# A transformer block kernel: first two mixers and the convolution part read each unit's sum from one PSUM bank, and GpSimd subtracts nothing

## The chip, the core and the metric

The kernel runs on one core of a Trainium2 chip, in one launch. The metric is device microseconds of that core; lower is better. Four compute engines work beside each other: PE (TensorE, the matrix engine, with its weight loads PEld beside its matmuls), DVE (VectorE), ACT (ScalarE) and POOL (GpSimd). SP (SyncE) issues the DMAs. Each engine runs its own instructions in order and waits on semaphores of the others. SBUF is the large on-chip memory; PSUM is the small one into which PE accumulates, used here as eight banks of 128 x 512 fp32.

## The reference, cut

256 tokens of width 1024 pass through two blocks. The first is a mixer (a pooling mixer, a chunked mLSTM with a short causal convolution, and a block attention side by side) and then a feed-forward net whose two halves pass a causal convolution over time:

```python
def causal_dwconv(x, w):
    xp = jnp.pad(x, ((0, 0), (K - 1, 0), (0, 0)))
    y = xp[:, 0:S] * w[0]
    for j in range(1, K):
        y = y + xp[:, j:j + S] * w[j]
    return y
# feed-forward, convolution part:  z = x @ w_up                  1024 -> 2 x 2816
#   h = silu(causal_dwconv(z)[gate]) * causal_dwconv(z)[up];  y = h @ w_down
```

The second block is two layers, each a gated feed-forward net (2816 wide, no convolution), a mixer (NSA attention in the first layer, HGRN in the second) and another gated feed-forward net. Everything is fp32, and nearly all of the work is products of the 256 tokens with weights that are used once.

## The kernel before

**Units.** All weights stream from HBM in units of 1 MB (`units`, made by `a_units` and `b_units`): 128 partitions x 8 x 256 or 2 x 1024 numbers. `get()` hands the next half unit to PE; by then units are loaded three ahead on SP's queue and halves split up to `ahead[0]` (5) ahead (`do_split`). Splitting writes a half as two numbers of reduced precision: ACT copies raw to `hi` (L264) and `lo = raw - hi` is a subtraction (L267) on DVE, or on POOL for the halves in `pool_halves`: five of the first mixer (table FP), every fifth of the convolution part and its last two (CF, CP), and the NSA mixer's last ones (`on_pool`), 30 in all. The hi buffers are six, the lo buffers three for each side, the raw buffers three.

**Products.** The activations XT are kept split as well, hi and lo side by side. There are two ways to multiply a kind "A" unit, whose weights are stationary:

- `gA` gives each half unit a PSUM bank of its own. For each of 8 slices k there is one matmul of hi weights on 512 columns (activations hi and lo) and one of lo weights on 256. The bank then holds two partial sums. `evA` (L434 to L445) adds them: ACT copies one to SBUF (`evs`, L441), DVE adds it to the other and writes z in SBUF (L442; with a scale L444 and L445). So a unit takes 32 matmuls, two banks and four evictions.
- `gZ`, used before in the HGRN mixer alone, gives both halves of a unit one bank. For each k there are three matmuls of 256 columns (lo weights on hi activations, hi on hi, hi on lo), all summed in PSUM. So a unit takes 48 matmuls and one bank, and whoever needs z reads the bank. Both pass through `bulk_mm` (L355).

PSUM tags psa and psb have two banks each; psS and psT have the other four.

**Where units are used.** In `first_mix`, `qk_m` multiplies two units and runs the mLSTM's short convolution on z (L704 to L706), `bulk_p` one and `bulk_a` two; `mmN` (L471) multiplies a narrow strip of gate weights in a psa bank. In `ffn` with conv=True each of ten iterations j takes a gate unit (psa) and an up unit (psb), then two halves of w_down (`mmD`, accumulators `acc`, 24 matmuls). `conv_z` runs three DVE operations on each half of z (L607 to L609), ACT takes Silu (L658), DVE multiplies (`times`, L626), and the product is split into H (L500 on ACT, L503 on DVE). At j = 0 the products have another form and the same three operations read a psS bank. At j = 10 `barrier` orders the following DVE subtractions behind `times`. In `nsa_mix`, `blocks` uses two units, `keys` two (ACT writes KH from z at L1112, DVE writes KL = z - KH at L1113, four of each), `bulk_q` four, later split in the same way into QS (L1136, L1137). Products L1097 go to psT banks and DVE reads them at L1100 (`vblk`).

**Order.** Each mixer's products run as generators that `drive` mixes with the small chains of attention and mLSTM; a scheduler then orders each engine's instructions. What stands in an engine's queue is fixed before the run.

Of the kernel before, what the change touches and what calls it, by code (L numbers as in the profile page):

```python
# [104 lines left out]
def _kern(ctx, tc, nc, A, out):  # L105
# [79 lines left out]
    for j in range(2):  # L185
        a_units(W, 1288 + 256 * j, 1)
        a_units(W, 1800 + 256 * j, 1, "B")
        a_units(W, 2312 + 256 * j, 1, "B")
    pool_halves.update(FP)
    b_units(A["w_out"], [0, 1, 2, 3])  # L190
    n0 = len(units)
    ffn_units(A["w_up"], 0, A["w_up"], DFF, A["w_down"], 2, 2)
    pool_halves.update(range(2 * n0 + CF[0], 2 * len(units) - 6, CF[1]))
    pool_halves.update(2 * len(units) + h for h in CP)
    for li in range(2):
        ffn_units(A["ffn1_w_gate_2"][li], 0, A["ffn1_w_up_2"][li], 0, A["ffn1_w_down_2"][li])
        if li == 0:
            W = A["nsa_w_in_2"]
            a_units(W, 1792, 1, "B")
            a_units(W, 2304, 1, "B")  # L200
            a_units(W, 1024, 2)
            a_units(W, 1536, 1)
            for kv in range(2):
                unit("c", kv, [16, 128])
            a_units(W, 2048, 1)
            narrow(W, 2560, 48)
            a_units(W, 0, 4)
            on_pool(len(units) - 9)
            b_units(A["nsa_w_out_2"], [0, 1, 2, 3])
        else:  # L210
            W = A["hgrn_w_in_2"]
            for j in range(4):
                for part in (1, 0, 3, 2) if j else (3, 2, 1, 0):
                    a_units(W, 1024 * part + 256 * j, 1, "A" if part < 2 else "B")
            b_units(A["hgrn_w_out_2"], [0, 1, 2, 3])
        ffn_units(A["ffn2_w_gate_2"][li], 0, A["ffn2_w_up_2"][li], 0, A["ffn2_w_down_2"][li])
# [379 lines left out]
    def ffn(XT, conv, half, finish):  # L596
        with tc.tile_pool(name=nm("ff"), bufs=2) as fp:
# [12 lines left out]
                return y  # L610

            def z_of(pool, ps, c0):
                return conv_z(evA(pool, ps, tag="cz", bufs=2), c0) if conv else evA(pool, ps)

            def turn(src):

# [18 lines left out]
            for j in range(11):  # L635
                sg = fp.tile([P, 2, 256], F32, tag="sg", name=nm("sg"))
                h = sg
                if j == 0:
                    pg, pu = mmB_first(XT)
                if j == 0 and conv:  # L640
                    zs = []
                    for n, ps in enumerate((pg, pu)):
                        zt = fp.tile([P, 2, 256], F32, tag="cz", bufs=2, name=nm("zt"))
                        for tt in range(2):
                            ACT.activation(zt[:, tt], ps[tt][:, 0:256], AF.Copy)
                        zs.append(conv_z(turn(zt), 22 * n))
                    ACT.activation(sg, zs[0], AF.Silu)
                    times(h, sg, zs[1])
                elif j == 0:
                    for tt in range(2):  # L650
                        ACT.activation(sg[:, tt], pg[tt][:, 0:256], AF.Silu)
                        times(sg[:, tt], sg[:, tt], pu[tt][:, 0:256])
                    h = turn(sg)
                else:
                    if conv and j == 10:
                        ahead[0] = SPL
                    zg = z_of(fp, mmA(XT), 2 * j)
                    ACT.activation(sg, zg, AF.Silu)  # L658
                    i = times(h, sg, z_of(fp, mmA(XT, psb), 22 + 2 * j))
                    if conv and j == 10:  # L660
                        barrier.append(i)
                H = fp.tile([P, 2, 2, 2, P], F32R, tag="H", bufs=2 + lag, name=nm("H"))
                split_to(H[:, :, :, 0, :], H[:, :, :, 1, :], h.rearrange("p c (t x) -> p c t x", t=2))
                ahead[0] = 5
                if j == 1:
                    acc = [new_acc(0), new_acc(1)]
                Hs.append(H)
                down(j - lag)
# [10 lines left out]
    def first_mix(XT, MT, W):  # L679
        with tc.tile_pool(name="m1", bufs=1) as mp:  # L680
# [6 lines left out]
            def qk_m():  # L687
# [9 lines left out]
                relative_bias(mp, rb)  # L697
                mT = []
                for u in range(2):
                    z = evA(mp, (yield from gA(XT)), tag="t2", bufs=4)  # L700
                    y = mp.tile([P, 2, 256], F32, tag="t2", bufs=4, name=nm("my"))
                    for c in range(2):
                        w = [vecs["m_conv"][:, 4 * j + 2 * u + c : 4 * j + 2 * u + c + 1] for j in range(4)]
# [14 lines left out]
                yield  # L718

            def bulk_p():  # L720
                ps = yield from gA(XT)
                d["zp"] = zp = mp.tile([P, 2, 272], F32, tag="zp", name="zp")
                POOL.memset(zp[:, :, 0:16], 0.0)
                evA(mp, ps, out=zp[:, :, 16:272])

            def bulk_a(u):
                d["zq", u] = zq = evA(mp, (yield from gA(XT)), tag="zq", bufs=2)

                sq = mp.tile([P, 2, 256], F32, tag="t2", bufs=4, name=nm("asq"))
                ACT.activation(sq, zq, AF.Square, scale=0.125)  # L730
# [290 lines left out]
    def nsa_mix(XT, MT, W):  # L1021
        with tc.tile_pool(name="m2", bufs=1) as mp:
# [20 lines left out]
            def blocks():  # L1043
# [8 lines left out]
                    for tt in range(2):  # L1052
                        ACT.activation(vv[br][:, tt], pss[br][tt][:, 0:256], AF.Copy)
                for kv in range(2):
                    z = evA(mp, (yield from gA(XT)), tag="zq", bufs=2)
                    blk = mp.tile([P, 16, 2, 2, 15], F32, tag="QS", bufs=2, name=nm("blk"))
                    for r in range(2):
                        rs = slice(64 * r, 64 * r + 64)
# [46 lines left out]
            KL = mp.tile([P, 4, 2, 256], F32R, name="KL")  # L1105

            def keys(br):
                z = evA(mp, (yield from gA(XT)), tag="zq", bufs=2)
                for r in range(2):
                    rs = slice(64 * r, 64 * r + 64)  # L1110
                    for o in (r, 1 - r):
# [12 lines left out]
                yield  # L1124

            def bulk_q(u):
                d["zq", u] = evA(mp, (yield from gA(XT)), scale=0.125, tag="zq", bufs=2)


            def group(u):  # L1130
# [455 lines left out]
```

## Time and profile before

| | before |
|---|---|
| median of 3 runs | 1419.66 us (1418.48 to 1422.54) |
| the profiled execution | 1419.54 us |
| its span, first to last instruction | 1417.7 us |
| granted TensorE clock, mean | 0.989 |
| PE busy | 1373.5 us, 97% |
| PEld busy | 1194.8 us, 84% |
| DVE busy | 971.8 us, 69% |
| ACT busy | 734.9 us, 52% |
| POOL busy | 116.6 us, 8% |

Starts and lengths are microseconds from the span's start. A line such as L267 is a line of the kernel before. "psa<-XT,hi" says that the operation writes a psa tile and reads XT and hi. Matmuls overlap, so their own durations add up to more than the time they take; the distance from one start to the next is the pace. "[6.26 <-DVE vblk L1100]" behind a row would be idle time of the engine ahead of it and what ended it. The granted clock is 1.00 at 2.4 GHz and 0.50 at 1.2 GHz.

### The profile page before, as it was taken

The page shows a single profiled execution, that of the slowest core. Times are in us where ns is not written, and L with a number is a line of the kernel's source. Part 1 is how long each engine was busy: PE and PEld are TensorE (multiplying, and loading weights), DVE is VectorE, ACT ScalarE, POOL GpSimd, SP SyncE. Part 2 cuts the span into 40 slices and gives each one's busy share as a digit, 9 for nine tenths or more (in the row PEclk, how much of TensorE's full clock was granted, in tenths as well). Part 3 has the DMA queues.
Part 4 walks back from the last instruction along what each step waited for, and adds up shares of the span by engine and source line. Part 5 has one row for each costly group of instructions (what it writes and reads, how often), then busy time and mean ns, then how long its engine had stood idle before and what let it go on. Part 6 is the DMA issues. An engine that isn't in the chain of part 4 may idle for free.

```text
span 1417.7 us, 20750 instructions
## 1 busy us (share of the span) xinstructions
PE 1373.5 (97%) x8121; PEld 1194.8 (84%) x8121; DVE 971.8 (69%) x1647; ACT 734.9 (52%) x1218; POOL 116.6 (8%) x95
## 2 busy tenths in 40 slices
PE   7899999998999999799999999999999999999997
PEld 6688888887888889688888888888889998888886
DVE  5865799997655776676855676665676666765574
ACT  5554554544555644576655564555555443645561
POOL 1320221220000003500000000000000000100000
PEclk9999999999999999899999999999999999999999
DMA  7523756654656665421555665555664442565560
GB/s 231 184 93 123 261 187 201 206 178 150 207 184 201 209 205 162 167 94 42 194 193 179 193 223 177 180 194 191 209 207 155 126 143 90 174 199 192 179 207 30
DMA packets 185425, 245.31 MB, mean 173 GB/s; under 512 B 7408, under 2 KB 164761, under 8 KB 185327
## 3 DMA queue, kind: packets, MB, share of 16 engines
q1 hardware_dynamic: 184511, 240.74, 52.0%
q0 software_dynamic: 816, 3.25, 0.6%
q8 instruction: 64, 1.05, 0.3%
q14 instruction: 34, 0.28, 0.1%
HBM read 242.89 MB, written 4.23 MB: 174 GB/s over the span
## 4 chain that ended last, share of the span: by engine, by line
PE 50%; issue 6%; DVE 1%; ACT 1%; POOL 1%; DVEq 0%; POOLq 0%; ACTq 0%
PE psa L355 19%; PE acc L355 13%; PE psb L355 12%; PE psb L1235 1%; PE psb L513 1%; PE psb L1237 0%; POOL rsr L536 0%; PE psT L1218 0%; PE psS L1189 0%; PE lev L1379 0%; PE psT L1220 0%; PE psb L1180 0%; PE psS L1147 0%; PE psS L1191 0%; ACT hi L264 0%
## 5 line engine op out<-in xcount | busy, mean ns | idle before, releaser
L267 DVE TENSOR_TENSOR lo<-raw,hi 128x1024 fp32r<-128x1024 f32 x398 | 492.5, 1243 | 252.2 <-ACT hi L264 251.1
L264 ACT ACTIVATE hi<-raw 128x1024 fp32r<-128x1024 f32 x428 | 448.5, 1055 | 330.2 <-PE psa L355 144.8
L355 PE MATMUL psa<-XT,hi 128*128 128x512 f32 (+1 forms) x1264 | 410.9, 375 | 3.2 <-DVE z L442 3.0
L355 PE MATMUL psa<-XT,lo 128*128 128x256 f32 x1136 | 322.2, 284 | 0.0
L355 PE MATMUL psb<-XT,hi 128*128 128x512 f32 x800 | 282.3, 393 | 0.0
L355 PE MATMUL acc<-hi,H 128*128 128x512 f32 x880 | 281.1, 392 | 0.0
L355 PEld LDWEIGHTS psa<-XT,hi 128*128 128x128 f32 x1264 | 230.3, 189 | 48.5 <-DVE z L442 4.2
L355 PE MATMUL psb<-XT,lo 128*128 128x256 f32 x800 | 223.3, 279 | 0.0
L355 PEld LDWEIGHTS psa<-XT,lo 128*128 128x128 f32 x1136 | 214.8, 189 | 3.8 <-issue 1.5
L355 PE MATMUL psa<-hi,XT 128*128 128x256 f32 (+1 forms) x928 | 197.4, 302 | 0.4 <-ACT XT L500 0.3
L355 PEld LDWEIGHTS acc<-hi,H 128*128 128x128 f32 x880 | 165.9, 189 | 35.3
L355 PEld LDWEIGHTS psb<-XT,hi 128*128 128x128 f32 x800 | 149.9, 187 | 35.9 <-DVE z L442 0.2
L355 PE MATMUL acc<-lo,H 128*128 128x512 f32 x440 | 173.8, 395 | 3.7 <-DVE lo L267 3.7
L355 PEld LDWEIGHTS psa<-hi,XT 128*128 128x128 f32 x928 | 150.8, 192 | 6.2 <-ACT XT L500 1.9
L355 PEld LDWEIGHTS psb<-XT,lo 128*128 128x128 f32 x800 | 149.9, 187 | 0.0
L355 PE MATMUL psa<-lo,XT 128*128 128x256 f32 (+1 forms) x464 | 131.2, 300 | 0.2 <-DVE lo L267 0.2
L355 PEld LDWEIGHTS acc<-lo,H 128*128 128x128 f32 x440 | 83.2, 189 | 20.8 <-DVE lo L267 4.1
L267 POOL TENSOR_TENSOR lo<-raw,hi 128x1024 fp32r<-128x1024 f32 x30 | 81.1, 2715 | 192.1 <-ACT hi L264 167.4
L355 PEld LDWEIGHTS psa<-lo,XT 128*128 128x128 f32 x464 | 89.4, 193 | 3.1 <-issue 1.0
L536 POOL TENSOR_TENSOR rsr<-var,mhalf 128x1 f32<-128x1 f32 x12 | 7.8, 647 | 796.5 <-ACT jk L574 796.5
L442 DVE TENSOR_TENSOR z<-psa,evs 128x256 f32<-128x256 f32 x116 | 48.3, 418 | 16.2 <-ACT evs L441 15.9
L500 ACT ACTIVATE H<-sg 128x512 fp32r<-128x512 f32 x51 | 31.7, 622 | 48.4 <-DVE sg L626 33.8
(350 smaller groups left out, 1294.5 us busy)
## 6 DMA issues: line engine op xcount, KB each, us to landing
raw<-in_ffn_w_gate_dram SPq DMA_DIRECT2D x44, 1024.0 KB, 5.1
raw<-in_ffn_w_up_dram SPq DMA_DIRECT2D x44, 1024.0 KB, 5.1
raw<-in_ffn_w_down_dram SPq DMA_DIRECT2D x44, 1024.0 KB, 4.9
raw<-in_w_up_dram SPq DMA_DIRECT2D x22, 1024.0 KB, 5.0
raw<-in_hgrn_w_in_dram SPq DMA_DIRECT2D x16, 1024.0 KB, 5.2
raw<-in_w_down_dram SPq DMA_DIRECT2D x11, 1024.0 KB, 4.9
raw<-in_nsa_w_in_dram SPq DMA_DIRECT2D x10, 1024.0 KB, 5.0
raw<-in_w_in_dram SPq DMA_DIRECT2D x9, 1024.0 KB, 5.1
```

The lines of the kernel that those rows point to most:

```text
L264: h = ACT.activation(hi, src, AF.Copy)
L267: i = (POOL if j in pool_halves else V).tensor_tensor(lo, src, hi.bitcast(F32), ALU.subtract)
L355: i = PE.matmul(o, l, r, start=start, stop=stop)
L442: V.tensor_tensor(zc, p4[:, :, 0, :], s, ALU.add)
L500: i = ACT.activation(hi, src, AF.Copy)
L513: ts = [PE.transpose(ps[:, j * P : (j + 1) * P], x[:, (q + j) * P : (q + j + 1) * P], ident) for j in range(w)]
L536: POOL.tensor_tensor(r[:, :n], src, mhalf[:, :n], ALU.pow)
L1235: PE.matmul(po5[:, 1, j % 2, br], T1[:, 2 * br + sb], vv[br][:, sb, vs], start=(sb == 0), stop=(sb == 1))
```

## The change

`pool_halves` stays empty: the 30 subtractions on POOL run on DVE. The five "A" units of the first mixer, the twenty of the convolution part and the eight of NSA (blocks, keys, bulk_q) go through `gZ` in place of `gA`, and `evA` is gone for them. Where z is used at once (mLSTM's convolution, `conv_z`, blocks, keys), DVE and ACT read the bank; in `bulk_p`, `bulk_a` and `bulk_q` one ACT copy of 128 x 512 takes z to SBUF. The gated feed-forward nets keep `gA` and `evA`. Behind L190 the changed kernel's line numbers are smaller by 1 to 4 (L355 is L351 there, L267 is L263).

```diff
@@ -186,12 +186,9 @@
         a_units(W, 1288 + 256 * j, 1)
         a_units(W, 1800 + 256 * j, 1, "B")
         a_units(W, 2312 + 256 * j, 1, "B")
-    pool_halves.update(FP)
     b_units(A["w_out"], [0, 1, 2, 3])
     n0 = len(units)
     ffn_units(A["w_up"], 0, A["w_up"], DFF, A["w_down"], 2, 2)
-    pool_halves.update(range(2 * n0 + CF[0], 2 * len(units) - 6, CF[1]))
-    pool_halves.update(2 * len(units) + h for h in CP)
     for li in range(2):
         ffn_units(A["ffn1_w_gate_2"][li], 0, A["ffn1_w_up_2"][li], 0, A["ffn1_w_down_2"][li])
         if li == 0:
@@ -205,7 +202,6 @@
             a_units(W, 2048, 1)
             narrow(W, 2560, 48)
             a_units(W, 0, 4)
-            on_pool(len(units) - 9)
             b_units(A["nsa_w_out_2"], [0, 1, 2, 3])
         else:
             W = A["hgrn_w_in_2"]
@@ -610,7 +606,7 @@
                 return y
 
             def z_of(pool, ps, c0):
-                return conv_z(evA(pool, ps, tag="cz", bufs=2), c0) if conv else evA(pool, ps)
+                return conv_z(ps, c0) if conv else evA(pool, ps)
 
             def turn(src):
 
@@ -654,9 +650,10 @@
                 else:
                     if conv and j == 10:
                         ahead[0] = SPL
-                    zg = z_of(fp, mmA(XT), 2 * j)
+                    mm = (lambda alloc: run(gZ(XT, alloc))) if conv else (lambda alloc: mmA(XT, alloc))
+                    zg = z_of(fp, mm(psa), 2 * j)
                     ACT.activation(sg, zg, AF.Silu)
-                    i = times(h, sg, z_of(fp, mmA(XT, psb), 22 + 2 * j))
+                    i = times(h, sg, z_of(fp, mm(psb), 22 + 2 * j))
                     if conv and j == 10:
                         barrier.append(i)
                 H = fp.tile([P, 2, 2, 2, P], F32R, tag="H", bufs=2 + lag, name=nm("H"))
@@ -697,7 +694,7 @@
                 relative_bias(mp, rb)
                 mT = []
                 for u in range(2):
-                    z = evA(mp, (yield from gA(XT)), tag="t2", bufs=4)
+                    z = yield from gZ(XT)
                     y = mp.tile([P, 2, 256], F32, tag="t2", bufs=4, name=nm("my"))
                     for c in range(2):
                         w = [vecs["m_conv"][:, 4 * j + 2 * u + c : 4 * j + 2 * u + c + 1] for j in range(4)]
@@ -718,13 +715,15 @@
                 yield
 
             def bulk_p():
-                ps = yield from gA(XT)
+                ps = yield from gZ(XT)
                 d["zp"] = zp = mp.tile([P, 2, 272], F32, tag="zp", name="zp")
                 POOL.memset(zp[:, :, 0:16], 0.0)
-                evA(mp, ps, out=zp[:, :, 16:272])
+                ACT.activation(zp[:, :, 16:272], ps, AF.Copy)
 
             def bulk_a(u):
-                d["zq", u] = zq = evA(mp, (yield from gA(XT)), tag="zq", bufs=2)
+                ps = yield from gZ(XT)
+                d["zq", u] = zq = mp.tile([P, 2, 256], F32, tag="zq", bufs=2, name=nm("zq"))
+                ACT.activation(zq, ps, AF.Copy)
 
                 sq = mp.tile([P, 2, 256], F32, tag="t2", bufs=4, name=nm("asq"))
                 ACT.activation(sq, zq, AF.Square, scale=0.125)
@@ -1052,7 +1051,7 @@
                     for tt in range(2):
                         ACT.activation(vv[br][:, tt], pss[br][tt][:, 0:256], AF.Copy)
                 for kv in range(2):
-                    z = evA(mp, (yield from gA(XT)), tag="zq", bufs=2)
+                    z = yield from gZ(XT)
                     blk = mp.tile([P, 16, 2, 2, 15], F32, tag="QS", bufs=2, name=nm("blk"))
                     for r in range(2):
                         rs = slice(64 * r, 64 * r + 64)
@@ -1105,7 +1104,7 @@
             KL = mp.tile([P, 4, 2, 256], F32R, name="KL")
 
             def keys(br):
-                z = evA(mp, (yield from gA(XT)), tag="zq", bufs=2)
+                z = yield from gZ(XT)
                 for r in range(2):
                     rs = slice(64 * r, 64 * r + 64)
                     for o in (r, 1 - r):
@@ -1124,7 +1123,9 @@
                 yield
 
             def bulk_q(u):
-                d["zq", u] = evA(mp, (yield from gA(XT)), scale=0.125, tag="zq", bufs=2)
+                ps = yield from gZ(XT)
+                d["zq", u] = zq = mp.tile([P, 2, 256], F32, tag="zq", bufs=2, name=nm("zq"))
+                ACT.activation(zq, ps, AF.Copy, scale=0.125)
 
 
             def group(u):
```

What this moves in the queues, at three places. First DVE at the end of the convolution part (before, then changed): z, the convolution's operations on cy, `times` (sg<-sg,cy), and the subtractions (lo) behind the barrier.

```order
L442 TENSOR_TENSOR z_3143<-psb_3126,evs_3147 128x256
L607 TENSOR_SCALAR cy_3150<-z_3143,vec_163 128x256
L608 SCALAR_TENSOR_TENSOR cy_3150<-z_3143,vec_156,cy_3150 128x255
L609 SCALAR_TENSOR_TENSOR cy_3150<-z_3143,vec_149,cy_3150 128x254
L626 TENSOR_TENSOR sg_3051<-sg_3051,cy_3150 128x512
L267 TENSOR_TENSOR lo_3164<-raw_3052,hi_3163 128x1024
L503 TENSOR_TENSOR H_3158<-sg_3051,H_3158 128x4x128
L267 TENSOR_TENSOR lo_3168<-raw_3052,hi_3167 128x1024
L267 TENSOR_TENSOR lo_3192<-raw_3161,hi_3191 128x1024
L267 TENSOR_TENSOR lo_3210<-raw_3161,hi_3209 128x1024
```

```order
L605 SCALAR_TENSOR_TENSOR cy_3356<-psb_3301,vec_149,cy_3356 128x254
L603 TENSOR_SCALAR cy_3356<-psb_3301,vec_163 128x256
L604 SCALAR_TENSOR_TENSOR cy_3356<-psb_3301,vec_156,cy_3356 128x255
L605 SCALAR_TENSOR_TENSOR cy_3356<-psb_3301,vec_149,cy_3356 128x254
L622 TENSOR_TENSOR sg_3241<-sg_3241,cy_3356 128x512
L263 TENSOR_TENSOR lo_3370<-raw_3243,hi_3369 128x1024
L499 TENSOR_TENSOR H_3364<-sg_3241,H_3364 128x4x128
L263 TENSOR_TENSOR lo_3374<-raw_3243,hi_3373 128x1024
L263 TENSOR_TENSOR lo_3378<-raw_3302,hi_3377 128x1024
L263 TENSOR_TENSOR lo_3382<-raw_3302,hi_3381 128x1024
L263 TENSOR_TENSOR lo_3398<-raw_3367,hi_3397 128x1024
L263 TENSOR_TENSOR lo_3416<-raw_3367,hi_3415 128x1024
```

Six subtractions stand behind `times` where four stood, as two of them were POOL's; the additions z are gone, and cy reads psb.

Next PE in NSA's second `keys`: the narrow gate product (L471 or L467), the products into psT banks (L1097 or L1096; `vblk` reads them), and the units of the following q products.

```order
L471 MATMUL psa_5413<-XT_3315,hi_5300 96x512 x4
L471 MATMUL psa_5413<-XT_3315,hi_5317 96x512 x4
L1097 MATMUL psT_5442<-cw_4989,hrep 128x128
L355 MATMUL psa_5452<-XT_3315,hi_5328 128x512
L355 MATMUL psa_5452<-XT_3315,lo_5329 128x2x128
...
L355 MATMUL psa_5452<-XT_3315,hi_5328 128x512
L355 MATMUL psa_5452<-XT_3315,lo_5329 128x2x128
L1097 MATMUL psT_5469<-cw_4989,hrep 128x128
L1097 MATMUL psT_5494<-cw_4989,hrep 128x128
L1097 MATMUL psT_5505<-cw_4989,hrep 128x128
L355 MATMUL psa_5477<-XT_3315,hi_5345 128x512
L355 MATMUL psa_5477<-XT_3315,lo_5346 128x2x128
```

```order
L467 MATMUL psa_5651<-XT_3521,hi_5530 96x512 x4
L467 MATMUL psa_5651<-XT_3521,hi_5547 96x512 x4
L1096 MATMUL psT_5680<-cw_5195,hrep 128x128
L1096 MATMUL psT_5715<-cw_5195,hrep 128x128
L351 MATMUL psa_5684<-XT_3521,lo_5559 128x256
L351 MATMUL psa_5684<-XT_3521,hi_5558 128x256 x2
...
L351 MATMUL psa_5684<-XT_3521,lo_5577 128x256
L351 MATMUL psa_5684<-XT_3521,hi_5576 128x256 x2
L1096 MATMUL psT_5747<-cw_5195,hrep 128x128
L1096 MATMUL psT_5753<-cw_5195,hrep 128x128
L351 MATMUL psa_5812<-XT_3521,lo_5610 128x256
L351 MATMUL psa_5812<-XT_3521,hi_5609 128x256 x2
```

Before, 16 matmuls lay between the first psT product and the other three, which stood together; now the first two stand together, and a whole unit (psa_5684, 48 matmuls) lies ahead of the other two.

Last DVE at the same place: KL (from z, now from psa_5573), `vblk` from the psT banks, and the subtractions that POOL made beside them.

```order
L442 TENSOR_TENSOR z_5398<-psa_5349,evs_5399 128x256
L442 TENSOR_TENSOR z_5398<-psa_5375,evs_5402 128x256
L1113 TENSOR_TENSOR KL<-z_5398,KH 64x2x256 x4
L1100 TENSOR_TENSOR vblk<-psT_5442,cst_4978 128x128 x2
L1100 TENSOR_TENSOR vblk<-psT_5469,cst_4978 128x128 x2
L1100 TENSOR_TENSOR vblk<-psT_5494,cst_4978 128x128 x2
L1100 TENSOR_TENSOR vblk<-psT_5505,cst_4978 128x128 x2
```

```order
L263 TENSOR_TENSOR lo_5577<-raw_5545,hi_5576 128x1024
L1112 TENSOR_TENSOR KL<-psa_5573,KH 64x2x256
L263 TENSOR_TENSOR lo_5610<-raw_5574,hi_5609 128x1024
L1112 TENSOR_TENSOR KL<-psa_5573,KH 64x2x256
L263 TENSOR_TENSOR lo_5655<-raw_5574,hi_5654 128x1024
L1112 TENSOR_TENSOR KL<-psa_5573,KH 64x2x256
L263 TENSOR_TENSOR lo_5663<-raw_5652,hi_5662 128x1024
L1099 TENSOR_TENSOR vblk<-psT_5680,cst_5184 128x128
L1112 TENSOR_TENSOR KL<-psa_5573,KH 64x2x256
L1099 TENSOR_TENSOR vblk<-psT_5680,cst_5184 128x128
L263 TENSOR_TENSOR lo_5688<-raw_5652,hi_5687 128x1024
L1099 TENSOR_TENSOR vblk<-psT_5715,cst_5184 128x128 x2
L263 TENSOR_TENSOR lo_5720<-raw_5685,hi_5719 128x1024
```

The subtractions of the next units now lie between the four KL and the vblk of the same queue.

## Rows read from the trace of the kernel before

**Rows 1.** Page, section 1: busy time, share of span, instructions of each engine.

```profile
PE 1373.5 (97%) x8121; PEld 1194.8 (84%) x8121; DVE 971.8 (69%) x1647; ACT 734.9 (52%) x1218; POOL 116.6 (8%) x95
```

**Rows 2.** PE's waits: engine, line waited for, total us, times, longest us.

```profile
PE psT L1097 <- DVE vblk L1100: 6.3, 1, 6.3
PE acc L355 <- DVE lo L267: 3.7, 1, 3.7
...
PE psa L355 <- DVE z L442: 3.0, 1, 3.0
PE psS L1189 <- DVE QS L1137: 2.2, 1, 2.2
...
PE psT L801 <- DVE rr L792: 1.2, 1, 1.2
PE psb L775 <- DVE sm L772: 1.2, 1, 1.2
```

**Rows 3.** Busy time by stretch: busy (instructions) of each engine, clock, DMA share, GB/s.

```profile
64.40:74.70 10.30, 10.30 (x35) 7.77 (x33) 5.63 (x13) 3.60 (x11) 0.00 (x0) 0.50 0.14 33
160.00:320.00 160.00, 159.96 (x853) 136.62 (x853) 148.74 (x226) 80.73 (x120) 36.16 (x13) 1.00 0.60 200
327.30:330.70 3.40, 3.04 (x7) 2.46 (x8) 3.40 (x5) 1.74 (x2) 0.00 (x0) 0.50 0.11 12
579.80:590.10 10.30, 8.53 (x31) 7.69 (x32) 3.62 (x12) 0.96 (x5) 5.65 (x3) 0.50 0.49 187
1083.50:1089.50 6.00, 6.00 (x52) 6.00 (x51) 5.17 (x12) 3.71 (x5) 0.00 (x0) 1.00 0.36 115
```

**Rows 4.** Chain of work in a gated feed-forward net (gA): start, us, what.

```profile
737.04 5.64 PE psa L355 x32
742.68 5.60 PE psb L355 x32
```

**Rows 5.** Chain of work in the HGRN mixer (gZ).

```profile
1084.90 5.40 PE psa L355 x45
...
1094.91 2.93 PE psa L355 x24
```

**Rows 6.** Groups by form, DVE and POOL: count, busy us, mean ns, idle before.

```profile
L267 DVE TENSOR_TENSOR lo<-raw,hi 128x1024 fp32r<-128x1024 f32 x398 | 492.5, 1243 | 252.2 <-ACT hi L264 251.1
L442 DVE TENSOR_TENSOR z<-psa,evs 128x256 f32<-128x256 f32 x116 | 48.3, 418 | 16.2 <-ACT evs L441 15.9
...
L267 POOL TENSOR_TENSOR lo<-raw,hi 128x1024 fp32r<-128x1024 f32 x30 | 81.1, 2715 | 192.1 <-ACT hi L264 167.4 <-DVE lo L267 12.5 <-DVE cy L609 12.2
```

**Rows 7.** Lines L607, L608: count, duration ns min/median/max, first and last start.

```profile
L607 DVE TENSOR_SCALAR cy<-z,vec x40: 339/353/2281, 168.6 to 324.4; 128x256 f32<-128x256 f32 x40
L607 DVE TENSOR_SCALAR cy<-psS,vec x4: 474/479/484, 161.4 to 164.6; 128x256 f32<-128x256 f32 x4
...
L608 DVE SCALAR_TENSOR_TENSOR cy<-psS,vec,cy x4: 472/474/474, 162.3 to 165.4; 128x255 f32<-128x255 f32 x4
```

**Rows 8.** Timeline of DVE and POOL around both keys: start, us, what.

```profile
560.71 2.79 DVE L1113 TENSOR_TENSOR KL<-z,KH 64x512 fp32r<-64x512 f32 x4 [0.16 <-ACT KH L1112]
...
572.19 8.73 DVE L1113 TENSOR_TENSOR KL<-z,KH 64x512 fp32r<-64x512 f32 x4 [1.03 <-ACT KH L1112]
...
591.57 2.43 DVE L1137 TENSOR_TENSOR QS<-z,QS 64x512 fp32r<-64x512 f32 x1 [1.04 <-ACT QS L1136]
...
575.27 10.17 POOL L267 TENSOR_TENSOR lo<-raw,hi 128x1024 fp32r<-128x1024 f32 x4 [1.16 <-ACT hi L264]
```

**Rows 9.** Timeline of DVE, POOL at the convolution part's end.

```profile
316.35 2.53 DVE L608 SCALAR_TENSOR_TENSOR cy<-z,vec,cy 128x255 f32<-128x255 f32 x1
...
326.39 1.22 DVE L267 TENSOR_TENSOR lo<-raw,hi 128x1024 fp32r<-128x1024 f32 x1
...
313.74 4.86 POOL L267 TENSOR_TENSOR lo<-raw,hi 128x1024 fp32r<-128x1024 f32 x2 [6.03 <-ACT hi L264]
```

**Rows 10.** Timeline of PE in the first mixer.

```profile
40.28 2.00 PE L471 MATMUL psa<-XT,hi 128*16 128x512 f32 x8
```

## The prediction

> **What bounds the kernel now.** I read the page's busy times first: PE is busy 97% of the span, DVE 69%, POOL 8% [rows 1]. So a DVE or POOL saving counts only where PE waits, and anything added to PE counts nearly in full. The second view is PE's waits [rows 2]. Six of them stand in code that the change touches: 6.3 us for vblk and 2.2 us for QS (NSA), 3.7 us for one subtraction (end of the convolution part), and 3.0, 1.2 and 1.2 us in the first mixer. The third is busy time by stretch [rows 3]. Through 160 us of the convolution part PE is busy 159.96 us, so nothing is to be won there, while DVE is busy 148.74 us (93%). And there are three stretches at the lower clock, 0.50 (1.2 GHz): 64.4 to 74.7, 327.3 to 330.7 and 579.8 to 590.1 us. PE had been idle just before the last two (the waits of 3.7 and 6.3 us), and there had been the two of 1.2 us before the first.
>
> **Products through gZ: the added cost.** A gA unit is 32 matmuls in 5.64 or 5.60 us [rows 4], mean 5.62. In the HGRN mixer gZ already runs: 45 matmuls in 5.40 us, 120.0 ns each, and 24 in 2.93 us, 122.1 ns [rows 5]. A gZ unit of 48 is then 5.76 us, or 5.86 at the second pace. There the weight loads are busy all the time (PEld 6.00 of 6.00 us [rows 3]), so the third load of each k does not hide wholly. 33 units x 0.14 us = **+4.6 us**. Bounds: 33 x 0.24 = +7.9, and 0 if only columns counted (768 for a k either way). I take 120.0, the longer piece. All of it is on PE's path.
>
> The Trainium skill ("TensorE: Matmul & The Clock Gate", section "Back-to-back issue gap") gives a matmul N/2.4 ns plus a fixed 2.5 ns at the upper clock. One more matmul for each of 16 k slices would then cost 0.04 us a unit, +1.3 us in all as an estimate by that page, and the sum would be 3.3 us lower. By its formula a matmul of 256 columns is 109 ns; the HGRN rows show 120 to 122, and the measurement decides.
>
> **Subtractions from POOL to DVE.** 30 leave POOL (2715 ns each) and 30 come to DVE (1243 ns) [rows 6]: +37 us of DVE. In return 66 additions z of 418 ns go, -28 us, with 66 ACT copies; seven ACT copies of a whole bank come back. In the convolution part, 853 matmuls in 160 us at 88 for an iteration (two units of 32 and 24 for w_down) are 9.7 iterations of 16.5 us; the changed one is 16.8 for PE. Its DVE work is then six subtractions (7.5 us), twelve convolution operations, and two of 128x512 (0.7 each, an estimate by size from KL and z). Operations on a PSUM bank have rows: at j = 0, L607 takes 479 ns and L608 473 [rows 7], so twelve cost 4 x 0.479 + 8 x 0.473 = 5.7 us. Sum 14.6 of 16.8 us, 87%: DVE stays under PE, cost 0.
>
> Against the change speaks the Trainium skill ("VectorE: DVE Perf Modes", section "Why PSUM operands drop a tier"): a PSUM operand takes an fp32 operation back to the single rate. The rows show it for the multiplication, 353 ns (median) from SBUF and 479 from PSUM; it makes 40 x 0.126 = 5 us more DVE work, which lies under PE by the 87%. Without that cover it would be 5 us.
>
> **End of the convolution part.** Before, L608 at 316.35 took 2.53 us while POOL subtracted (313.74 to 318.60), against 0.473; so the chain to `times` ran late, its subtraction started at 326.39 [rows 9], and PE waited 3.7 us for it, then ran slow: 3.04 us of busy PE at 0.50 did some 1.5 us of work. After, POOL is quiet, and the z additions and their ACT copies are out of the chain (four of 0.42 us on DVE). I step through the new queue: the up unit done at 318.4, six convolution operations to 321.1, `times` 321.85, the first lo 323.0, H, then lo at 324.85, 326.0 and 327.1. PE needs these at about 323.8, 325.2, 326.5 and 327.9 (estimates from the durations above). Six subtractions stand behind the barrier and not four; the slack is 0.3 to 0.8 us. The wait and the slow stretch go: -3.7 - 1.5 = **-5.2 us**. Bounds: 0 if the chain is late anyway, -5.2.
>
> **NSA.** In the second `keys` four KL took 8.73 us from 572.19, with POOL subtracting from 575.27 to 585.44; in the first, four took 2.79 us [rows 8]. The vblk behind them came late, PE waited 6.3 us, and the clock then stood at 0.50 for 10.3 us, in which PE was busy 8.53 us [rows 3]: about 4.3 us lost. QS took 2.43 us at 591.57 beside another POOL subtraction, and PE waited 2.2 us. After, KL takes 0.7 us, but four subtractions (1.24 each) stand between them: about 7.7 us, hardly less than 8.73. What decides is PE's own order: a whole unit (5.76 us) now stands between the second and third psT product. vblk is done near 578, needed near 581. A new wait is likely: that unit reuses a psa bank and waits for the ACT copy of the narrow product, 1.5 us by my stepping; 1 more is allowed for QS, which now follows its subtractions. -6.3 - 2.2 - 4.3 + 2.5 = **-10.3 us**. Bounds: -12.8 without new waits; -4 if new waits reach 4.5 us and the clock still falls.
>
> **First mixer.** PE reaches the narrow product at 40.28 and runs it for 2.00 us at once [rows 10], then waits 3.0 us for z. After, its bank is that of the first gZ unit, held until DVE's last convolution read (near 42.4), so the wait of 2.1 us stands ahead of the product, and 0.8 us behind it: the 3.0 us only moves. At the two of 1.2 us I get 1.75 and 0.4 us. The five subtractions from POOL join DVE here. Net **-1 us**, bounds -5.4 (all three waits gone) and +3 (one such wait more). The slow stretch at 64.4 I leave as it is.
>
> **Sum.** +4.6 - 5.2 - 10.3 - 1 = -11.9. The profiled execution took 1419.54 us (1.8 us of it outside the span), within 0.1 us of the median 1419.66. 1419.5 - 11.9 = 1407.6, say **1408 us**.
>
> **Rivals.**
> - *The first slow stretch goes too.* PE's 10.30 us at 0.50 [rows 3] hold some 5.2 us of loss. For: the waits before it get shorter by about 1 us. Against: two remain. 1402.5 us.
> - *The clock falls in NSA all the same, or in a new place.* For: the stretch at 64.4 shows that waits of 1.2 us can stand before a fall, and I expect 1.5 us at the psa bank. It gives 4.3 to 5.2 us back: 1413.
> - *POOL was not the cause.* If KL and QS keep their long times with POOL quiet, or the subtractions now in DVE's queue delay vblk by the same amount, NSA gains nothing, nor the convolution part's end; gZ remains: 1419.5 + 4.6 - 1 = 1423. It needs vblk some 3 us later than I step it. Against: KL at 560.71 took 0.70 us each.
> - *Slower: DVE becomes the bound of the convolution part.* The point is (16.8 - 7.5 - 1.4) / 12 = 0.66 us for each of the twelve operations that read PSUM while PE writes the other banks. At 0.80 us it costs 12 x 0.14 x 10 = 17 us: 1425. Against: the 473 and 479 ns were measured with PE at work; but only on psS banks, twelve in all. Its DVE is at 93% before, so no other slack is known.
> - That the change does not do what it says can hardly be: the queue of POOL and the matmul counts show it. gZ at another pace lies in my range: 1403 to 1411.
>
> **How the numbers follow.** Chances: 1408 0.54, 1402.5 0.14, 1413 0.18, 1423 0.08, 1425 0.06. A measurement of this kernel can tell about 0.3% (4.3 us) from no change: 1415.4 to 1423.9. Faster takes the first two and most of the third, 0.82; same is the rest of the third and most of 1423, 0.10; slower 0.08. The range of 8 in 10 leaves out both of the last, and the ends of the second: 1401 to 1417.
>
> **What would show it.** Right: no POOL row with L267's subtraction; the waits for vblk and for the convolution part's lo gone or under 1 us; no 0.50 in 570 to 595 nor near 327; four KL under 1 us each; gZ units of 5.7 to 5.9 us in the chain; twelve convolution operations of 0.47 us with DVE under 90% there. Wrong: PE idle in 170 to 310 us behind DVE (the slower rival), or a new wait of several us for a psa bank at the narrow products.

## The result and the profile after

| | before | changed |
|---|---|---|
| median of 5 runs each | 1421.52 us (1418.48 to 1422.54) | 1405.71 us (1401.31 to 1410.73) |
| ratio, 95% interval | | 0.9887 (0.9859 to 0.9914) |
| the profiled execution, span | 1419.54, 1417.7 us | 1410.73, 1408.8 us |

The change is faster by 1.1% (0.9 to 1.4). The profiled execution of the changed kernel happens to be the slowest of its five, so its trace shows 8.8 us of gain where the medians show 15.8.

First the busy times of the changed kernel's page (they answer [rows 1]). POOL's 81 us of subtractions are gone; PE has 528 matmuls more.

```profile
PE 1376.0 (98%) x8649; PEld 1221.9 (87%) x8649; DVE 950.4 (67%) x1611; ACT 722.5 (51%) x1159; POOL 35.8 (3%) x65
```

Next PE's waits (engine, line waited for, total us, times, longest us), as in [rows 2]; here `vblk`, `lo` behind acc, QS and rr are gone, and hc (a late step of the first mixer, L893 of before) has grown from 0.5 to 1.7 us. L470 is ACT's copy of a narrow product, L703 the mLSTM's convolution, L771 is L772 of before.

```profile
PE psa L351 <- ACT nr L470: 2.2, 2, 1.5
...
PE psa L467 <- DVE my L703: 1.9, 1, 1.9
PE psb L509 <- DVE hc L892: 1.7, 1, 1.7
PE psb L774 <- DVE sm L771: 1.1, 1, 1.1
```

The chain of work through one iteration of the convolution part (start, us, what), which answers [rows 4, 5]: a gate unit, an up unit, a w_down unit. gZ's 48 matmuls take 5.75 us in the convolution part too.

```profile
193.87 5.75 PE psa L351 x48
199.62 5.76 PE psb L351 x48
205.38 5.50 PE acc L351 x24
```

In NSA every KL takes 0.69 us, and `vblk` starts at 578.6, ahead of the third psT product at 582.4 (these lines answer [rows 8]: count, duration min/median/max, first and last start).

```profile
L1112 DVE TENSOR_TENSOR KL<-psa,KH x8: 683/688/694, 559.7 to 578.9; 64x512 fp32r<-64x512 f32 x8
L1099 DVE TENSOR_TENSOR vblk<-psT,cst x8: 282/284/292, 578.6 to 583.4; 128x128 f32<-128x128 f32 x8
```

Busy time by stretch (columns as in [rows 3]). The lower clock is gone at the end of the convolution part (323 to 333 us) and in NSA (570 to 595). In the first mixer there are two stretches where there was one.

```profile
42.50:51.00 8.50, 7.83 (x36) 5.80 (x34) 5.78 (x9) 4.30 (x7) 0.00 (x0) 0.60 0.75 240
90.10:105.40 15.30, 14.89 (x64) 12.16 (x65) 6.15 (x27) 5.92 (x20) 0.00 (x0) 0.55 0.09 36
160.00:320.00 160.00, 159.96 (x1161) 151.79 (x1160) 131.35 (x199) 75.62 (x83) 0.00 (x0) 1.00 0.63 211
323.00:333.00 10.00, 10.00 (x51) 8.42 (x51) 8.29 (x12) 0.73 (x2) 0.00 (x0) 1.00 0.06 9
570.00:595.00 25.00, 23.50 (x181) 22.29 (x180) 22.13 (x62) 18.30 (x35) 0.00 (x0) 1.00 0.69 232
```

To see where the time went, four marks that both traces have (line, count, duration min/median/max, first and last start): the convolution's operations at j = 0, `blk` in NSA, NSA's last product with its gate (oo), and HGRN's qq. Of before:

```profile
L1061 DVE TENSOR_TENSOR blk<-z,posT x8: 1034/1054/3031, 546.6 to 558.2; 64x480 f32<-64x480 f32 x8
L1247 DVE TENSOR_TENSOR oo<-oo,wo x16: 416/422/426, 609.2 to 675.0; 128x256 f32<-128x256 f32 x16
L1344 DVE SCALAR_TENSOR_TENSOR qq<-qq,om,psa x8: 472/476/479, 1088.1 to 1170.8; 128x256 f32<-128x256 f32 x8
```

Of the changed kernel:

```profile
L603 DVE TENSOR_SCALAR cy<-psS,vec x4: 476/478/484, 165.1 to 168.3; 128x256 f32<-128x256 f32 x4
L1060 DVE TENSOR_TENSOR blk<-psa,posT x8: 1040/1055/1078, 547.2 to 556.2; 64x480 f32<-64x480 f32 x8
L1248 DVE TENSOR_TENSOR oo<-oo,wo x16: 415/423/426, 602.1 to 667.1; 128x256 f32<-128x256 f32 x16
L1345 DVE SCALAR_TENSOR_TENSOR qq<-qq,om,psa x8: 475/477/481, 1078.9 to 1161.6; 128x256 f32<-128x256 f32 x8
```

| stretch, us | before | changed | difference |
|---|---|---|---|
| start to first operation at j = 0 (161.4, 165.1): first mixer | 161.4 | 165.1 | +3.7 |
| to the first blk (546.6, 547.2): convolution part, gated net | 385.2 | 382.1 | -3.1 |
| to the last qq (1170.8, 1161.6): NSA, a gated net twice, HGRN | 624.2 | 614.4 | -9.8 |
| to the span's end (1417.7, 1408.8) | 246.9 | 247.2 | +0.3 |

Most of the difference of the third line arises in NSA: from the first blk to the last oo it is 128.4 against 119.9 us, -8.5.

### The profile page after: what moved, and what is told of

It reads as the page before. It is cut to its first block, busy times and chain, and to the rows that moved or that the text cites. A ratio compares the mean times of both kernels' runs of the same rounds, so it can differ in the third digit from the quotient of the medians.

```text
span 1408.8 us, 21630 instructions
## 1 busy us (share of the span) xinstructions
PE 1376.0 (98%) x8649; PEld 1221.9 (87%) x8649; DVE 950.4 (67%) x1611; ACT 722.5 (51%) x1159; POOL 35.8 (3%) x65
## 4 chain that ended last, share of the span: by engine, by line
PE 87%; issue 7%; DVE 2%; DMA 1%; ACT 1%; POOL 1%; SPq 0%; POOLq 0%; DVEq 0%; ACTq 0%
PE psa L351 36%; PE acc L351 23%; PE psb L351 20%; PE psb L509 1%; PE psb L1236 1%; POOL rsr L532 1%; DMA x<-in_x_dram 1%; ACT hi L260 1%; DVE lo L263 1%; PE psT L1219 1%; PE psS L1069 1%; PE psb L1238 0%; PE psS L1190 0%; DMA pst<-in_nsa_cmp_pos_dram 0%; DMA raw<-in_w_in_dram 0%
## 5 line engine op out<-in xcount | busy, mean ns | idle before, releaser
L263 DVE TENSOR_TENSOR lo<-raw,hi 128x1024 fp32r<-128x1024 f32 x428 | 522.5, 1226 | 267.5 <-ACT hi L260 264.8
L351 PE MATMUL psa<-XT,hi 128*128 128x256 f32 (+1 forms) x1632 | 414.4, 329 | 0.0
L351 PE MATMUL psa<-XT,lo 128*128 128x256 f32 x1136 | 323.3, 285 | 2.2 <-ACT nr L470 2.2
L351 PEld LDWEIGHTS psa<-XT,hi 128*128 128x128 f32 x1632 | 276.6, 190 | 30.3 <-issue 0.7
L351 PE MATMUL psb<-XT,hi 128*128 128x512 f32 (+1 forms) x960 | 283.7, 356 | 0.0
L351 PE MATMUL acc<-hi,H 128*128 128x512 f32 x880 | 280.6, 392 | 0.0
L351 PE MATMUL psb<-XT,lo 128*128 128x256 f32 x800 | 223.8, 280 | 0.0
L351 PEld LDWEIGHTS psa<-XT,lo 128*128 128x128 f32 x1136 | 215.1, 189 | 6.7 <-ACT nr L470 3.3
L351 PE MATMUL psa<-hi,XT 128*128 128x256 f32 (+1 forms) x928 | 197.6, 303 | 0.8 <-ACT XT L496 0.6
L351 PEld LDWEIGHTS acc<-hi,H 128*128 128x128 f32 x880 | 165.3, 188 | 34.9
L351 PEld LDWEIGHTS psb<-XT,hi 128*128 128x128 f32 x960 | 169.3, 188 | 28.7
L351 PE MATMUL acc<-lo,H 128*128 128x512 f32 x440 | 172.6, 392 | 0.0
L351 PEld LDWEIGHTS psa<-hi,XT 128*128 128x128 f32 x928 | 151.0, 192 | 7.3 <-ACT XT L496 2.5
L351 PEld LDWEIGHTS psb<-XT,lo 128*128 128x128 f32 x800 | 149.9, 187 | 0.0
L351 PE MATMUL psa<-lo,XT 128*128 128x256 f32 (+1 forms) x464 | 130.4, 298 | 0.2 <-DVE lo L263 0.2
L351 PEld LDWEIGHTS acc<-lo,H 128*128 128x128 f32 x440 | 82.8, 188 | 16.4
L351 PEld LDWEIGHTS psa<-lo,XT 128*128 128x128 f32 x464 | 89.1, 192 | 2.2 <-DVE lo L263 0.5
L496 ACT ACTIVATE XT<-psb 128x512 fp32r<-128x512 f32 (+1 forms) x46 | 23.7, 530 | 48.1 <-PE psb L509 47.9
L655 ACT ACTIVATE sg<-z 128x512 f32<-128x512 f32 x40 | 25.2, 631 | 40.5 <-DVE z L438 40.2
L499 DVE TENSOR_TENSOR H<-sg,H 128x512 fp32r<-128x512 f32 x51 | 35.0, 686 | 5.6 <-ACT H L496 5.6
```

The lines of the kernel that those rows point to most:

```text
L263: i = (POOL if j in pool_halves else V).tensor_tensor(lo, src, hi.bitcast(F32), ALU.subtract)
L351: i = PE.matmul(o, l, r, start=start, stop=stop)
L496: i = ACT.activation(hi, src, AF.Copy)
L499: V.tensor_tensor(lo, src, hi.bitcast(F32), ALU.subtract)
```

## The experiments

Twelve runs follow, two of them repeats; runs taken side by side share their runs of the kernel before. Times are medians. A difference in us is the ratio's, applied to the median of those runs of before, unless it is said to be of medians or of a trace.

**The three parts alone, and one undone.** Each kernel undoes the change in all parts but one, or in one. The pieces (first mixer, as an example):

```diff
-                    z = yield from gZ(XT)
+                    z = evA(mp, (yield from gA(XT)), tag="t2", bufs=4)
...
+    pool_halves.update(FP)
```

> The change in the first mixer alone (five units through gZ, its five subtractions on DVE); convolution part and NSA as before. My account: the waits of 3.0, 1.2 and 1.2 us only move (2.0 us ahead of the narrow product, 0.8 behind it), gZ costs 5 x 0.14 us, and stretches at the lower clock come and go from run to run: the median between -4 and +3 us of before, first convolution operation of the FFN at 158 to 166 us. Rival, the first mixer as a source of the gain: -4 to -8 us in every run. Rival, a cost: +3 us or more in every run.

Measured: 1420.56 us over 12 runs (1413.93 to 1425.72), ratio 0.9987 (0.9973 to 1.0000). A gain of 0 to 4 us that varies by 12 us from run to run. The waits at the narrow product moved as expected: 1.8 us ahead of it and 0.8 behind it for the 3.0. One wait is new in size: 1.8 us for hc, where the kernel before has 0.5.

> The change in the convolution part alone. My account: 20 units x 0.14 us = +2.8 us, the wait of 3.7 us at its end and the slow stretch behind it (1.5 us) gone: -2.4 us, -1 to -4, no wait of acc for lo. Rival, DVE bound by PSUM reads: PE idle behind DVE in 180 to 320 us, +5 us or more.

Measured: 1417.56 us, ratio 0.9965 (0.9952 to 0.9979), -5.0 us. The wait of acc for lo is gone and PE waits for DVE nowhere in 180 to 320 us. The sign and the mechanism held; the runs gave more than 2.4 us, and by the four marks its trace shows 3.1 us in this stretch (382.1 against 385.2).

> The change in NSA alone. My account: -9 to -11 us (the waits of 6.3 and 2.2 us and the slow stretch of 10.3 us gone, 8 x 0.14 us added, one new wait of 1.5 us for the narrow product's ACT copy). Rival, the gain hangs on the stages ahead of it: under -5 us.

Measured: 1411.82 us, ratio 0.9924 (0.9908 to 0.9939), -10.8 us. The waits for vblk and QS are gone from its list, the waits of the untouched parts (3.7, 3.0, 1.2, 1.1 us) and the new one for nr stand in it:

```profile
PE acc L354 <- DVE lo L266: 3.7, 1, 3.7
...
PE psa L354 <- DVE z L441: 3.0, 1, 3.0
...
PE psa L354 <- ACT nr L473: 1.5, 1, 1.5
```

> The whole change without its part in the first mixer. If the parts add up: -2.4 - 10 = -12.5 us, 1408 us beside 1420.5, so 2 to 3 us above the changed kernel's median and below its slowest run. Rival, the first mixer's part costs time: below the changed kernel, under 1404 us.

Measured: 1407.03 us (1404.39 to 1407.73), ratio 0.9894 (0.9876 to 0.9913), -15 us beside its own runs of before. The three parts add up roughly (-1.9 - 5.0 - 10.8 = -17.7, where the whole change has -16.1, and -14.4 when run again, below). Whether the first mixer's part is kept or not decides nothing that these runs can tell.

**POOL or gZ?** The change does two things at once. One kernel only moves the subtractions (the pool_halves lines go, nothing else), the other only changes the products (gZ, the pool_halves lines stay).

> Only the 30 subtractions move from POOL to DVE; all units stay with gA and evA. If POOL's work beside DVE is what stretched KL, QS and the convolution: KL 0.7 us and QS 0.7 us, the wait for vblk 2 to 4 us in place of 6.3 (the subtractions stand in the same queue, and PE's order is the old one), the end of the convolution part without most of its 3.7 us: -6 to -10 us. Rival, the whole gain is POOL's and gZ a pure cost: -13 us or more. Rival, POOL was not the cause: within 2 us of before.

Measured: 1406.94 us, ratio 0.9901 (0.9887 to 0.9915), -14.1 us. In total this is the rival's number: without POOL's subtractions gA and evA give nearly all of it, at 5.61 us a unit. KL (first) takes 686 ns, and no wait for vblk or QS is left. (PE's order moved here as well: 16 matmuls now lie between the second psT product and the last two, where before had none and the changed kernel has 48.) One new wait stands at the start of the convolution part (171.33 us), for a hi half, with the lower clock behind it:

```profile
L1110 DVE TENSOR_TENSOR KL<-z,KH x8: 677/686/689, 555.4 to 570.8; 64x512 fp32r<-64x512 f32 x8
```

```profile
PE psa L351 <- ACT hi L260: 4.6, 1, 4.6
```

> The 33 units through gZ, but POOL keeps its 30 subtractions. If any POOL subtraction beside DVE stretches it: KL over 2 us, convolution operations of over 2 us in places, and the gain falls to -2 to -6 us (the new order of the psT products still takes most of the wait for vblk). Rival, only operations with two SBUF inputs are stretched, and KL and the convolution now read PSUM: KL 0.7 us beside POOL, QS still over 2 us, -8 us or more.

Measured: 1407.39 us, ratio 0.9905 (0.9884 to 0.9926), -13.5 us, and again the rival's number. POOL subtracts for 18.8 us on end in NSA, and KL beside it takes 0.69 us; it reads z from the bank now. QS, which reads zq from SBUF, is still stretched, to 1.9 us at the worst, and PE waits 2.5 us for it, with the clock at 0.57 from 582 to 586 us. Rows of KL and QS by line, and of POOL by time:

```profile
L1116 DVE TENSOR_TENSOR KL<-psa,KH x8: 682/689/695, 557.0 to 573.4; 64x512 fp32r<-64x512 f32 x8
```

```profile
L1142 DVE TENSOR_TENSOR QS<-zq,QS x8: 685/686/1887, 580.8 to 639.8; 64x512 fp32r<-64x512 f32 x8
```

```profile
563.29 18.80 POOL L267 TENSOR_TENSOR lo<-raw,hi 128x1024 fp32r<-128x1024 f32 x8 [10.13 <-ACT hi L264]
```

The convolution shows the same: its second operation took up to 2.64 us in the kernel before, where z lies in SBUF, and at most 0.486 in gZ_pool, where it reads the bank and POOL subtracts as before:

```profile
L608 DVE SCALAR_TENSOR_TENSOR cy<-z,vec,cy x40: 473/484/2640, 170.0 to 324.7; 128x255 f32<-128x255 f32 x40
```

```profile
L608 DVE SCALAR_TENSOR_TENSOR cy<-psa,vec,cy x20: 475/483/486, 168.2 to 316.2; 128x255 f32<-128x255 f32 x20
```

So either half of the change frees KL, and together they give hardly more than either. Whether it is the place of KL's input that does it in gZ_pool, the next kernel tells: gZ_pool with that one thing put back in the text (the scheduler then moved PE's products too, see below):

```diff
-                z = yield from gZ(XT)
+                ps = yield from gZ(XT)
+                z = mp.tile([P, 2, 256], F32, tag="zq", bufs=2, name=nm("kz"))
+                ACT.activation(z, ps, AF.Copy)
```

> The 33 units through gZ, POOL keeps its 30 subtractions, and in NSA's keys ACT first copies the bank to SBUF, so that KL has two SBUF inputs again. If it is the place of the inputs that saved KL (0.69 us each beside POOL where one input was PSUM): KL goes to 2 us and more while POOL subtracts, and vblk comes 4 us or more later. Rival, KL was saved because POOL's subtractions fell at another time: KL stays at 0.7 us.

Measured: 1409.02 us, ratio 0.9903 (0.9882 to 0.9925). The time is not told apart from gZ_pool's, but KL is: with z in SBUF the same four KL take 10.06 us while POOL subtracts, and PE waits 3.7 us for vblk again. Timeline of DVE, of POOL, and PE's wait:

```profile
571.80 10.06 DVE L1118 TENSOR_TENSOR KL<-kz,KH 64x512 fp32r<-64x512 f32 x4
```

```profile
565.82 20.61 POOL L267 TENSOR_TENSOR lo<-raw,hi 128x1024 fp32r<-128x1024 f32 x8 [10.04 <-ACT hi L264]
```

```profile
PE psT L1100 <- DVE vblk L1103: 3.7, 1, 3.7
```

The same four marks in the traces of these kernels (us; one trace each) show that equal totals are not equal gains:

| trace | first mixer | convolution part, gated net | NSA, first blk to last oo | the rest |
|---|---|---|---|---|
| before | 161.4 | 385.2 | 128.4 | 742.7 |
| changed | 165.1 | 382.1 | 119.9 | 741.7 |
| no_pool_gA | 155.3 | 387.2 | 122.7 | 740.8 |
| gZ_pool | 160.7 | 382.1 | 120.6 | 742.3 |
| gZ_pool_zcopy | 161.9 | 383.0 | 122.0 | 740.6 |
| conv_gA (below) | 159.0 | 387.9 | 119.8 | 740.3 |

In NSA the quiet POOL alone gives 5.7 us, gZ alone 7.8, both 8.5. In the convolution part gZ alone gives the whole 3.1 us and the quiet POOL alone loses 2.0: the wait at the part's end goes, the one at its start comes. What no_pool_gA makes up in the first mixer (6.1 us) is in good part less time at the lower clock there (about 1.7 us lost against 5.1), which differs from run to run (see below). And KL's slowness is not the bulk of NSA's loss once PE's order has changed: gZ_pool_zcopy, with KL slow again, is 1.4 us longer there than gZ_pool and keeps 6.4 us.

**gA in the convolution part, without POOL.** The changed kernel with `evA` and `mmA` put back in `z_of` and the loop of `ffn`.

> The changed kernel, but the convolution part's 20 units with gA and evA as before, without POOL. PE saves 20 x 0.14 = 2.8 us; DVE does per iteration 6 x 1.23 + 4 x 0.42 + 12 x 0.45 + 1.4 = 15.9 us of 16.5. If that fits: 1 to 3 us below the changed kernel, with a wait of about 1 us at the part's end. Rival, DVE at 96% is late again and again: 2 us or more above the changed kernel, PE waits for lo or z in 170 to 330 us.

Measured: 1409.88 us, ratio 0.9919 (0.9906 to 0.9932), at the slow end of the changed kernel's own runs (1401.3 to 1411.1); by the marks its convolution part and gated net take 5.8 us more (387.9 against 382.1). DVE keeps up from the second iteration on: no wait for lo or z after 176 us, none at the part's end, and DVE is busy 125.37 of 140 us (90%; busy time by stretch). The 2.8 us and more are lost in the first iteration, where PE waits 4.76 us for a bank and then runs at the lower clock:

```profile
180.00:320.00 140.00, 140.00 (x737) 119.73 (x737) 125.37 (x212) 74.22 (x104) 0.00 (x0) 1.00 0.59 196
```

```profile
175.11 0.77 PE L351 MATMUL psa<-XT,hi 128*128 128x512 f32 x1 [4.76 <-DVE z L438]
```

A gA unit fills both psa banks, so the next gate unit has to wait until z is added from the first; with gZ it takes the other bank. That alone does not make the wait: before has gA here too and no such wait. Here ACT's first copy `evs` of that unit stood behind a `hi` that waited 10.98 us for its weights, and z came only at 174.54; in before the two copies ran at 165.34 and 167.56, ahead of such a wait. The changed kernel has the same late weights (ACT idle for 10.36 us until 176.18) and PE does not wait. The wait of no_pool_gA at 171.33 stands at the same place, behind the same late `hi`.

```profile
170.63 1.06 ACT L260 ACTIVATE hi<-raw 128x1024 fp32r<-128x1024 f32 x1 [10.98 <-DMA raw<-in_w_up_dram]
```

The number fits the rival, its reason (DVE at 96%) does not.

**The bank held in the first mixer.** ACT copies the mLSTM's units to SBUF, and the convolution reads them there:

```diff
-                    z = yield from gZ(XT)
+                    ps = yield from gZ(XT)
+                    z = mp.tile([P, 2, 256], F32, tag="t2", bufs=4, name=nm("mz"))
+                    ACT.activation(z, ps, AF.Copy)
```

> The changed kernel, but ACT copies the mLSTM's two gZ units whole to SBUF and the short convolution reads them there, so the bank is free after 0.6 us. If the bank held by the convolution's reads is what stops PE at the narrow product: the wait of 1.9 us there goes and the median falls by 1 to 3 us. Rival, the wait only moves to the next product (ACT's copy of the narrow product comes no earlier): within 1 us.

Measured: 1403.12 us (1400.48 to 1405.61), ratio 0.9876 (0.9858 to 0.9895). The narrow product starts at 40.59 with no wait ahead of it, against 42.06 and 1.85 us of waiting in the changed kernel:

```profile
40.59 2.01 PE L467 MATMUL psa<-XT,hi 128*16 128x512 f32 x8
```

```profile
42.06 3.10 PE L467 MATMUL psa<-XT,hi 128*16 128x512 f32 x8 [1.85 <-DVE my L703]
```

It ran again beside the changed kernel, and with the narrow products moved to a psb bank (`pr = psb()` in `mmN`):

> The changed kernel once more, beside the other two on the same chip: 1401 to 1411 us, with the mean clock of each run going down as its time goes up (the slow stretches of the first mixer come and go); all other stages as in its first profile within 1 us.

> qk_copy once more beside the changed kernel: if the bank held by the convolution's reads is a real wait, 1.5 to 3 us below the changed kernel in the median of the same call; rival, the difference of the first calls was the come and go of slow stretches: within 1 us.

> qk_copy, and the narrow products (first mixer and NSA) take a psb bank, so the unit behind them need not wait for ACT's copy of the narrow product. Both waits of psa for nr (1.5 us in NSA, up to 0.8 in the first mixer) go: 1 to 3 us below qk_copy, near 1400 to 1402. Rival, a psb bank is held as long by others and the wait only changes its name: within 1 us of qk_copy.

Measured side by side: the changed kernel 1407.99 us, ratio 0.9899 (0.9882 to 0.9917), and in its new trace each of the four stretches is within 0.5 us of the first; qk_copy 1404.73, 0.9880 (0.9867 to 0.9893); qk_copy_nr **1402.14**, 0.9861 (0.9846 to 0.9876). qk_copy is 3 us lower by medians (1403.12 against the changed kernel's first 1405.71, taken apart, and 1404.73 against 1407.99), but its intervals overlap those of the changed kernel. qk_copy_nr's lies below that of the changed kernel beside it, so it beats before and the changed kernel; from qk_copy it is not told apart by the intervals, though NSA is 2.4 us shorter in its trace (117.4 against 119.8). Its list has no wait for nr or my any more, and the stretch at 42.5 us is at full clock; the later one remains:

```profile
42.50:51.00 8.50, 8.50 (x72) 8.34 (x71) 7.85 (x14) 5.21 (x7) 0.00 (x0) 1.00 0.81 268
85.00:100.30 15.30, 14.66 (x62) 11.93 (x63) 6.17 (x26) 5.83 (x19) 0.00 (x0) 0.55 0.10 41
```

## Why the prediction was right, and where it was off

It gave 1408 us (1401 to 1417); the medians are 1405.71 and 1407.99. The gain itself was put too low (11.9 us against 16.1 and 14.4), and that the time came out so near owes 2 us to the base (last point).

- **gZ's pace** was right: 5.76 us was taken from HGRN, 5.75 and 5.76 were measured in the convolution part. Against gA's 5.62 that is +0.14 us a unit. The formula of the Trainium skill ("TensorE: Matmul & The Clock Gate", section "Back-to-back issue gap") would have made it +0.04; no run shows that. That section of the Trainium skill gives this formula for a single matmul in isolation, and the prediction applied it to a stream.
- **Convolution operations from PSUM**: 479 ns was taken from four rows, and the changed kernel shows 478 to 479 for the 40 multiplications and under 490 for the other operations. DVE fell from 148.74 busy us to 131.35 in 160 to 320 us (82%). The slower rival has nothing left.
- **End of the convolution part and gated net**: +2.8 - 5.2 = -2.4 forecast, -3.1 in the trace, and conv_only gave -5.0 by its runs and -3.1 in its trace.
- **NSA**: +1.1 - 10.3 = -9.2 forecast, -9.8 in the trace (-8.5 between blk and oo), -10.8 in nsa_only's runs. The new wait for the narrow product's copy was forecast at 1.5 us and is 1.50; KL takes 0.69.
- **The reason given for the NSA gain is confirmed only in part.** I named the quiet POOL as what frees KL, and PE's new order as what decides. gZ_pool loses the wait for vblk with POOL at work, so the quiet POOL was not needed: KL reading one input from PSUM is freed as well. How much is the order's stays open. In gZ_pool_zcopy 24 matmuls of a unit lie between the second psT product and the last two (before has none, no_pool_gA 16, gZ_pool and the changed kernel 48), and with KL slow PE waits 3.7 us; 24 more at 0.12 us would have left some 0.8 us of that (an estimate from this trace). So the order may well cover most of a slow KL, as I said; the order's 48 matmuls with a slow KL were not tried. The prediction had no rival in which either half of the change alone gives nearly the whole time.
- **First mixer**: +0.7 - 1 = -0.3 forecast, +3.7 in the trace. At the narrow product the waits came as stepped through (2.1 and 0.8 us forecast, 1.85 and 0.68 measured). At the two of 1.2 us, forecast as 1.75 and 0.4, one is gone (rr) and one is 1.08 (sm); that hc would grow to 1.7 was not seen. What was mis-sized is the time at the lower clock: I left the slow stretch as it was. In this trace it went from 64.4 and two others came, with 8.5 x 0.40 + 15.3 x 0.45 = 10.3 us lost against 5.1 (length times what the clock lacks of 1.00, an estimate). That this is no cost of the change itself shows in the traces of other kernels with the same first mixer. Four have it as before (before, conv_only, nsa_only, first_undone): 160.5 to 163.0 us, with 5.1 to 6.9 lost at the lower clock by the same reckoning. Four have it changed (the changed kernel twice, first_only, conv_gA): 158.5 to 165.2 us, with 1.7 to 10.3 lost. Without that loss all eight take 155 to 157 us, so the forecast of about nothing holds for the code, and the rest is the clock. Over the changed kernel's eleven runs the fastest (1401.31) has a mean clock of 0.998, the slowest (1411.09) 0.990, and 0.008 of 1405 us is 11 us. The run-to-run spread is thus of the clock's size, and my rivals at 1402.5 and 1413 us are near its two ends; that the time fell between them is in part luck.
- **The base**: the sum went from 1419.5 us, but the kernel before has medians of 1421.5 to 1423.0 with more runs. That is 2 to 3.5 us of the gain that no step of the sum holds.

What starts a slow stretch in the first mixer is not settled. With the waits at 40 to 46 us taken away the stretch at 42.5 went, in the one trace of qk_copy_nr and both of qk_copy. But the same code with the same waits goes either way: before has a wait of 3.0 us there and no slow stretch behind it, conv_only the same wait and one; first_only and conv_gA have the changed kernel's waits at 42 to 46 us and none there. The later stretch begins at the wait for hc in six of the seven traces in which that wait is 1.7 us or more (not in conv_gA), and in none of the seven in which it is 0.5 to 1.3. No kernel took that wait away. Rows of conv_only, of first_only, and two of conv_gA:

```profile
45.00:49.00 4.00, 3.23 (x10) 2.78 (x11) 3.93 (x6) 1.50 (x3) 2.42 (x1) 0.57 0.60 177
```

```profile
88.00:92.00 4.00, 4.00 (x18) 2.99 (x18) 3.16 (x13) 1.81 (x6) 0.00 (x0) 0.57 0.19 78
```

```profile
65.00:72.00 7.00, 7.00 (x28) 5.10 (x27) 4.91 (x11) 5.54 (x15) 0.00 (x0) 0.51 0.38 146
90.10:105.40 15.30, 15.15 (x116) 13.38 (x117) 10.01 (x34) 10.24 (x28) 0.00 (x0) 1.00 0.18 64
```

## What to carry to other kernels

Where a second engine is given part of an elementwise load, look at what the first engine's operations take while both run: 81 us on POOL cost PE two long waits that stood under other names, and the place of one operand (PSUM or SBUF) decided whether the operation beside POOL was stretched. When a change does two things, price each as if the other were absent; here either alone gave 14 us and both gave 14 to 16. Compare such kernels stage by stage: the two halves reached the same total from different stages. And a PSUM bank that a chain of vector operations reads is held until the last of them: where PE was next in line for that bank, one ACT copy that frees it early took PE's wait of 1.85 us away (the gain in time, some 3 us by medians, is not clear of the spread).

## What was not expected of the hardware

- A DVE subtraction of 64x512 with both inputs in SBUF takes 0.69 us alone and about 2.5 beside a POOL subtraction (10.06 us for four); with one input in PSUM it takes 0.69 us beside the same POOL work. The Trainium skill ("SBUF — State Buffer", section "Who interferes with whom") says so: a DVE instruction with two SBUF inputs contends with a GpSimd instruction that reads SBUF, one with at most one such input does not, outside the modes in which DVE takes both ports. These traces agree with it, by 0.689 us against 2.5. One input in SBUF was not always safe: L607, which multiplies z from SBUF by a column of numbers, took up to 2.28 us in the kernel before (median 0.353) and at most 0.485 from the bank in gZ_pool, and a DVE copy of 128x16 from SBUF took 2.44 us beside POOL in gZ_pool and 0.16 beside it in gZ_pool_zcopy. The rows do not show in which mode these ran.
- A run's time broadly followed its mean granted clock (1401.3 us at 0.998, 1411.1 at 0.990), with the same instructions: a spread of 10 us over eleven runs, where the kernel before has 6 over all of its own (1418.10 to 1424.40).
